# Block products for three of the five down-projection steps at the end of a two-layer decoder step

## The chip, the core and the metric

The program runs on one NeuronCore of a Trainium2 chip. The core has a matrix engine (TensorE, PE in the profile; its weight loads are PEld), VectorE (DVE), ScalarE (ACT), GpSimd (POOL) and SyncE (SP), each with an instruction queue of its own that runs in order, and 16 DMA engines, on which transfers issued from SP, ACT and POOL run. Matmuls write to PSUM, which has 8 banks of 512 f32 per partition. The metric is the device time of one execution in microseconds; less is better.

## The reference

Two groups of tokens (a prompt of 1024 and 8 samples) go through two layers that share all weights. Each layer has a mixer and then a SwiGLU feed-forward block, with norms before and after and a residual sum. What this change touches is the feed-forward block:

```python
def swiglu(h, w_gu, w_down):
    gate, up = jnp.split(h @ w_gu, 2, axis=-1)
    return (jax.nn.silu(gate) * up) @ w_down
...
h = h + rmsnorm(swiglu(rmsnorm(h, g[2]), w_gu[l], w_down[l]), g[3])
```

`w_gu` is 1024 x 5632 and `w_down` 2816 x 1024, in float32.

## The kernel before

Activations lie transposed: features on the 128 partitions, tokens along the free dimension. The tokens are cut into two groups: group 0 holds 512 prompt tokens, group 1 the other 512 and the 8 samples, 520 in all, worked as two halves of `h` = 260. Every float32 product is made as three products of rounded parts: a tile is split into a rounded tile (a cast on ScalarE) and the remainder (a subtraction on VectorE), and high x high, high x low and low x high are added up in PSUM. `split_w` (L196), `split_to` (L226) and `split` in `gate_up_w` (L509) do this for weights and activations; a weight tile of 128 x 512 is 256 KB, loaded on SP's queue.

The 22 feature tiles of 128 are cut into `PARTS` of 5, 5, 4, 4 and 4 (L582). For each part, the gate and up products of its tiles are made, then the part's contribution to the down projection is added to `R`, eight tiles of 128 output features by 520 tokens.

The program's end is the feed-forward block of group 1 in layer 1, class `ffn_w` (L584). Its first four feature tiles are plain (`gate_up_q`, L468). The other 18 go through `gate_up_w` (L493): the 1024 x 2 x 260 problem of one tile's gate and up is seen as 2 x 2 blocks and made with seven products instead of eight (Winograd's form). The seven need four sums of weight blocks, which `weight_sums` (L557) makes earlier, in DRAM, with POOL transfers: plain copies and accumulating ones, eight per part, for all 22 tiles. Each is released by a token, a ScalarE copy of one column of something just computed into a tile of three buffers (tag "rr"), and a POOL copy of that (L571, L572), so the transfers are spread over the feed-forward block of group 0 in layer 1 (L1648 to L1650). They also need sums of activation blocks, made once by `sums_w` (L295).

The down step of a part in `ffn_w.part` (L608) is plain: for each of the eight output tiles it loads and splits the part's rows of `w_down` (two loads where the part has five tiles), makes three matmuls per feature tile and token half (L638), and adds both halves to `R` on VectorE (L647). The fifth part's step is `down_rows` (L651), which works in two groups of tokens, makes the norm's statistics as it goes, and turns the result to rows and stores it.

PSUM in this last part is one pool of four tags with two buffers each, all eight banks (`Q`, L87, L1670). `gate_up_w` takes one bank of each tag, a plain down step two of them for each output tile. Weight buffers come from `spl` and `raws` (L593, L599), which in parts 1 to 4 also borrow from two other pools.

Instructions are put in order by a scheduler with priorities in program order; `weave` (L174) interleaves generators by their weights, and so sets these priorities. In layer 0, the recurrence of group 1 (`a1.core`) is woven with the first feed-forward part of group 0 (`f0.part(0)`) at L1632. At the start, 14 mask tiles `mf` (L1579) are made by POOL in a pool `tpool` of three buffers, and the page table is loaded to a tile of its own (L1609) and made into row indices, which the gathers of L1000 use.

Of the kernel before, what the change touches and what calls it, by code (L numbers as in the profile page):

```python
# [9 lines left out]
F32 = mybir.dt.float32  # L10
# [8 lines left out]
P = 128  # L19
# [5 lines left out]
def tile_decoder(  # L25
# [56 lines left out]
    def N():  # L82
        return npool.tile([P, WID], F32, tag="n", name=nm("n"))
# [14 lines left out]
    def M(dt=F32):  # L98
        return mpool.tile([P, 2, WID], dt, tag="m", name=nm("m"))
# [21 lines left out]
    def small(shape, dt=F32, tag="sm", bufs=None):  # L121
        return spool.tile(shape, dt, tag=tag, name=nm(tag), bufs=bufs)
# [42 lines left out]
    def drain(*gens):  # L165
        for g_ in gens:
            for _ in g_:
                pass
# [5 lines left out]
    def weave(*streams):  # L174
        drain(mixed(*streams))
# [50 lines left out]
    def split_to(dst, src):  # L226
        nc.scalar.copy(dst[0], src)  # L227
        nc.vector.tensor_sub(dst[1], src, dst[0].bitcast(F32))  # L228
# [261 lines left out]
        split_to((mt[:, 0, :n], mt[:, 1, :n]), sg[:, :n])  # L490
        return mt, last

    def gate_up_w(l, f, ops, spl, raws):  # L493

        h, n = PW[1], NG[1]
        part, o = part_of(f)
        gate, up = f * P, DFF + f * P
        src = [
            (w_gu[l][0:512, gate : gate + P], 0), (sums[l][part][0][:, o : o + P], 4), (sums[l][part][1][:, o : o + P], 5),
            (w_gu[l][512:D, gate : gate + P], 1), (sums[l][part][2][:, o : o + P], 6), (sums[l][part][3][:, o : o + P], 2),  # L500
            (w_gu[l][512:D, up : up + P], 3),
        ]

        def weight(j):
            r = raws()
            nc.sync.dma_start(r, src[j][0].rearrange("(k p) m -> p k m", p=P))
            return r.rearrange("p k m -> p (k m)")

        def split(src):  # L509
            w = spl()  # L510
            nc.scalar.copy(w[:, 0, :], src)  # L511
            nc.vector.tensor_sub(w[:, 1, :], src, w[:, 0, :].bitcast(F32))  # L512
            return w

        def product(ps, j, first=False):
            w = split(weight(j))
            i = src[j][1]
            for k in range(4):
                x = ops[k][i]
                for wi, (wj, xi) in enumerate(((0, 0), (0, 1), (1, 0))):  # L520
                    nc.tensor.matmul(  # L521
                        ps[:, :h], w[:, wj, k * P : (k + 1) * P], x[:, xi, :],
                        start=(first and k == 0 and wi == 0), stop=(k == 3 and wi == 2), skip_group_check=True,
                    )
# [6 lines left out]
        nc.scalar.activation(pc[:, :h], pb[:, :h], AF.Copy, scale=-1.0)  # L531
# [12 lines left out]
        nc.vector.tensor_mul(sg[:, :h], sg[:, :h], pb[:, :h])  # L544
        nc.vector.tensor_mul(sg[:, h:n], sg[:, h:n], gt[:, h:n])
        mt = M(F32R)
        split_to((mt[:, 0, :n], mt[:, 1, :n]), sg[:, :n])
        return mt

    sums = {}  # L550
# [3 lines left out]
            if f0 <= f < f0 + nf:  # L554
                return i, (f - f0) * P

    def weight_sums(l, parts, after):  # L557

        for i in parts:
            f0, nf = PARTS[i]  # L560
            w = nf * P
            s1, s2, s3, s4 = (tc.dram_tile([512, w], F32, name=nm("wsum")) for _ in range(4))
            sums.setdefault(l, {})[i] = (s1, s2, s3, s4)
            a11, a12 = (w_gu[l][r : r + 512, f0 * P : f0 * P + w] for r in (0, 512))
            a21, a22 = (w_gu[l][r : r + 512, DFF + f0 * P : DFF + f0 * P + w] for r in (0, 512))
            for d, a, add in (
                (s3, a11, False), (s1, a21, False), (s3, a21, True), (s1, a22, True),
                (s2, s3, False), (s2, a22, True), (s4, s2, False), (s4, a12, True),
            ):
                tok = small([P, 1], tag="rr")  # L570
                nc.scalar.copy(tok, after())  # L571
                mark = nc.gpsimd.tensor_copy(small([P, 1], tag="mk", bufs=1), tok)  # L572
                with tc.issue_after(mark.ins):
                    if add:
                        nc.gpsimd.dma_start(d, a, accum_op=ALU.add)
                    else:
                        nc.gpsimd.dma_start(d, a, max_dma_last_dim=4 * w)
                yield

    htok, done = [], []  # L580

    PARTS = [(0, 5), (5, 5), (10, 4), (14, 4), (18, 4)]  # L582

    class ffn_w:  # L584


        def __init__(self, l, x, plain):
            self.g, self.l, self.x, self.ops, self.plain, self.n, self.r, self.pi = 1, l, x, [], plain, 0, 0, 0
            self.R = self.acc = None
            self.half = []  # L590
            self.sums = sums_w(x, self.ops)

        def spl(self):  # L593
# [12 lines left out]
            return wraw.tile([P, 4, P], F32, tag="w", name=nm("w"))  # L606

        def part(self, pi):  # L608
            l, n, h = self.l, NG[1], PW[1]
            f0, nf = PARTS[pi]  # L610
            last = pi == len(PARTS) - 1
            mids = []
            for j in range(nf):
                self.pi = pi
                if f0 + j < self.plain:
                    mt, ins = gate_up_q(l, f0 + j, self.x)
                    mids.append(mt)
                    with tc.issue_after(ins.ins):
                        for _ in range((1, 2, 1, 0)[j]):
                            next(self.sums, None)  # L620
                else:
                    mids.append(gate_up_w(l, f0 + j, self.ops, self.spl, self.raws))
                yield
            if pi == 0:
                self.R = R_one()
            if last:
                with tc.issue_after(done[-1].ins):
                    nc.scalar.preload_act_table_set("natural_log_exp_and_others")
                yield from self.down_rows(mids, f0, nf)
                return  # L630
            for m in range(ND):
                w = split_w(w_down[l], f0, nf, m * P)
                pp = [Q(2 * (m % 2) + a) for a in range(2)]
                for k in range(nf):
                    wh, wl = w[k]
                    for wi, (wt, xi) in enumerate(((wh, 0), (wh, 1), (wl, 0))):
                        for a in range(2):
                            nc.tensor.matmul(  # L638
                                pp[a][:, :h], wt, mids[k][:, xi, a * h : (a + 1) * h],
                                start=(k == 0 and wi == 0), stop=(k == nf - 1 and wi == 2),  # L640
                            )
                for a in range(2):
                    d = self.R[m][:, a * h : (a + 1) * h]
                    if pi == 0:
                        nc.scalar.copy(d, pp[a][:, :h])
                    else:
                        nc.vector.tensor_add(d, d, pp[a][:, :h])  # L647
                if m % 2:
                    yield
# [960 lines left out]
    nc.sync.dma_start(ptb, page_table.rearrange("b j -> (b j)").partition_broadcast(P))  # L1610
# [95 lines left out]
```

## Time and profile before

| what | value |
|---|---|
| median of 3 runs | 2442.65 us (2439.48 to 2443.6) |
| the profiled execution, its own time | 2441.46 us |
| its span, first to last instruction | 2439.7 us |
| mean granted clock of TensorE | 0.998 |
| packets of DMA, bytes | 496726, 360.33 MB |

The profile is one execution. A line of its views gives the engine, the source line, the operation and the tiles (out <- in), the shapes and the count. Busy times of PE are modelled ends of pipelined matmuls, so the length of a row of matmuls in the chain, divided by their number, is the cost of one. "Idle before" is the time in which an engine stood still before such an instruction, and what ended it. The chain of work that ended last is followed back from the last instruction, at each step to what released it.

### The profile page before, as it was taken

The numbers are of one execution on the slowest core, as the hardware profiler recorded it, in microseconds if no ns is written. First come the engines' busy times: TensorE is split into PE (matmuls) and PEld (weight loads), VectorE is DVE, ScalarE is ACT, GpSimd is POOL, SyncE is SP. The second block draws the span as 40 slices with busy tenths as digits, with TensorE's granted clock in tenths as the row PEclk, the third lists the DMA queues.
The fourth block names the chain that finished last, engine by engine and source line by source line (L and its number), as shares of the span: only waits on it lengthen the run. The fifth ranks groups of instructions, "written<-read, shape, count | busy, mean of one in ns | idle before, by whom it ended". The sixth has DMA issues, their size and how long they took to land.

```text
span 2439.7 us, 40660 instructions
## 1 busy us (share of the span) xinstructions
PE 2410.5 (99%) x15483; PEld 2140.8 (88%) x15483; DVE 1561.0 (64%) x2688; ACT 1205.8 (49%) x2371; POOL 106.3 (4%) x167
## 2 busy tenths in 40 slices
PE   8999999999999999999999999999999999999998
PEld 6888988888877887999999989877787898999998
DVE  5777556765775676555544585677678548755665
ACT  5547544444444454555433454555454445554445
POOL 3000000000000000011111100021000000000000
PEclk9999999999999999999999999999999999999999
DMA  6353252254643446685778966544454234474542
GB/s 189 97 157 107 74 156 84 71 172 121 181 135 95 139 147 209 175 222 149 181 198 211 247 183 193 162 146 136 127 156 130 81 121 125 125 195 144 151 140 75
DMA packets 496726, 360.33 MB, mean 148 GB/s; under 512 B 19181, under 2 KB 443738, under 8 KB 496530
## 3 DMA queue, kind: packets, MB, share of 16 engines
q1 hardware_dynamic: 477864, 303.15, 41.7%
q0 software_dynamic: 18560, 54.53, 9.3%
q8 instruction: 122, 2.00, 0.3%
q14 instruction: 74, 0.61, 0.1%
q10 hardware_dynamic: 106, 0.04, 0.0%
HBM read 327.83 MB, written 75.96 MB: 166 GB/s over the span
## 4 chain that ended last, share of the span: by engine, by line
PE 92%; DVE 3%; DMA 2%; ACT 1%; issue 1%; SPq 0%; DVEq 0%; ACTq 0%; POOLq 0%; POOL 0%
PE mm L220 63%; PE q L521 7%; PE q L638 4%; PE q L479 2%; PE mm L1064 2%; PE s L914 1%; PE s L873 1%; PE s L1422 1%; PE s L1247 1%; PE mm L850 1%; PE q L722 1%; PE s L1461 1%; PE mm L823 1%; PE s L900 1%; DMA b<-qd 1%
## 5 line engine op out<-in xcount | busy, mean ns | idle before, releaser
L220 PE MATMUL mm<-x,ws 128*128 128x260 f32 (+1 forms) x7776 | 1330.5, 330 | 0.0
L220 PEld LDWEIGHTS mm<-x,ws 128*128 128x128 f32 x7776 | 1149.4, 188 | 143.1 <-issue 8.0
L206 ACT CAST ws<-w 128x512 fp32r<-128x512 f32 x704 | 414.8, 590 | 674.0 <-PE mm L220 556.4
L207 DVE TENSOR_TENSOR ws<-w,ws 128x512 fp32r<-128x512 f32 x704 | 456.6, 652 | 259.9 <-ACT ws L206 254.8
L220 PE MATMUL mm<-m,ws 128*128 128x512 f32 (+1 forms) x2112 | 391.9, 342 | 0.3 <-DVE r L416 0.3
L220 PEld LDWEIGHTS mm<-m,ws 128*128 128x128 f32 x2112 | 323.3, 188 | 47.0 <-issue 3.3
L512 DVE TENSOR_TENSOR ws<-w,ws 128x512 fp32r<-128x512 f32 x126 | 86.5, 691 | 59.7 <-ACT ws L511 57.0
L521 PE MATMUL q<-y,ws 128*128 128x260 f32 x864 | 112.9, 283 | 0.0
L511 ACT CAST ws<-w 128x512 fp32r<-128x512 f32 x126 | 78.0, 621 | 68.2 <-PE q L638 27.3
L521 PEld LDWEIGHTS q<-y,ws 128*128 128x128 f32 x864 | 107.6, 188 | 0.0
L638 PE MATMUL q<-m,ws 128*128 128x260 f32 x864 | 104.7, 282 | 0.0
L638 PEld LDWEIGHTS q<-m,ws 128*128 128x128 f32 x864 | 103.8, 188 | 0.3 <-ACT hT L454 0.2
L416 DVE TENSOR_TENSOR r<-r,mm 128x512 f32<-128x512 f32 (+1 forms) x96 | 66.0, 688 | 56.6 <-PE mm L220 55.5
L260 DVE TENSOR_SCALAR t<-mm 128x512 f32<-128x512 f32 (+1 forms) x74 | 51.2, 691 | 63.7 <-PE mm L220 63.7
L770 DVE TENSOR_TENSOR t<-t,mm 128x512 f32<-128x512 f32 (+1 forms) x66 | 45.5, 690 | 67.8 <-PE mm L220 67.2
L264 DVE TENSOR_TENSOR t<-t,t 128x512 f32<-128x512 f32 (+1 forms) x66 | 45.8, 693 | 65.7 <-ACT t L263 65.7
L521 PE MATMUL q<-x,ws 128*128 128x260 f32 x648 | 86.3, 282 | 0.0
L521 PEld LDWEIGHTS q<-x,ws 128*128 128x128 f32 x648 | 81.3, 188 | 0.0
L227 ACT CAST m<-t 128x512 fp32r<-128x512 f32 (+1 forms) x88 | 54.9, 624 | 24.7 <-DVE t L770 16.7
L1000 POOL DMA_INDIRECT c<-in_cache_sb_k,pidx x16 | 16.7, 1042 | 1120.8 <-DMA vsc<-c 910.9
L283 DVE TENSOR_TENSOR st<-st,n 128x512 f32<-128x512 f32 (+1 forms) x91 | 62.2, 691 | 3.1 <-ACT n L282 1.5
L228 DVE TENSOR_TENSOR m<-t,m 128x512 fp32r<-128x512 f32 (+1 forms) x88 | 60.9, 692 | 2.8 <-ACT m L227 1.6
(356 smaller groups left out, 2579.9 us busy)
## 6 DMA issues: line engine op xcount, KB each, us to landing
w<-in_w_gu SPq DMA_DIRECT2D x334, 256.0 KB, 3.3
w<-in_w_down SPq DMA_DIRECT2D x160, 256.0 KB, 2.9
w<-in_w_in_a SPq DMA_DIRECT2D x80, 256.0 KB, 2.9
wsum<-in_w_gu POOLq DMA_DIRECT2D x18, 1024.0 KB, 9.3
w<-wsum SPq DMA_DIRECT2D x72, 256.0 KB, 3.8
w<-in_w_o SPq DMA_DIRECT2D x64, 256.0 KB, 2.8
wsum<-in_w_gu POOLq DMA_DIRECT2D x12, 1280.0 KB, 10.9
w<-in_w_mem_kv SPq DMA_DIRECT2D x32, 256.0 KB, 3.2
```

The source lines that it names most:

```text
L206: nc.scalar.copy(ws[:, 0, :n, :], raw[:, :n, :])
L207: nc.vector.tensor_sub(ws[:, 1, :n, :], raw[:, :n, :], ws[:, 0, :n, :].bitcast(F32))
L220: nc.tensor.matmul(ps[:, a, : PW[g]], wt, xt[k][:, xi, o : o + PW[g]], start=(k == 0 and wi == 0), stop=(k == nk - 1 and wi == 2),)
L227: nc.scalar.copy(dst[0], src)
L228: nc.vector.tensor_sub(dst[1], src, dst[0].bitcast(F32))
L260: nc.vector.tensor_scalar(sv(x, g), pv(ps, g), -44.0, None, op0=ALU.max)
L283: nc.vector.tensor_add(acc[:, :n], acc[:, :n], t[:, :n])
L416: nc.vector.tensor_add(dst, dst, pv(ps, g))
L511: nc.scalar.copy(w[:, 0, :], src)
L512: nc.vector.tensor_sub(w[:, 1, :], src, w[:, 0, :].bitcast(F32))
L521: nc.tensor.matmul(ps[:, :h], w[:, wj, k * P : (k + 1) * P], x[:, xi, :], start=(first and k == 0 and wi == 0), stop=(k == 3 and wi == 2), ...
L638: nc.tensor.matmul(pp[a][:, :h], wt, mids[k][:, xi, a * h : (a + 1) * h], start=(k == 0 and wi == 0), stop=(k == nf - 1 and wi == 2),)
```

## The change

The down steps of parts 1, 2 and 3 go to a new method `down_w`, which sees the first four feature tiles of the part as two blocks of rows, the 1024 output features as two blocks of columns and the tokens as two halves, and makes seven products. It runs in two passes of two output tiles (and the two that lie 512 features further); each pass takes all eight PSUM banks. The fifth tile of part 1 is added by plain matmuls (`slice_of`).

The activation sums that this needs are made in `gate_up_w` at the end of the second tile of each pair (`put_sum`), in place and in a pool whose tiles grow from 2048 to 2080 bytes. The weight sums of `w_down` are made in DRAM by `down_sums`, 24 POOL transfers of 512 KB, woven with `a1.core` and `f0.part(0)` in layer 0. `weight_sums` leaves out the columns of the four plain tiles. In the last part, the gate and up of the next part's first tile is put ahead of the down steps of parts 2 and 3. The page table and an index tile move to `tpool`.

```diff
-    def gate_up_w(l, f, ops, spl, raws):
+    def gate_up_w(l, f, ops, spl, raws, pair=None):
...
-        sg = T()
+        sg = T() if pair is None else N()
...
         mt = M(F32R)
+
+        def put_sum(dst, d, a, b):
+            nc.vector.tensor_sub(d, a, b)
+            split_to((dst[:, 0], dst[:, 1]), d)
+
+        if not pair:
+            w = n if pair is None else h
+            split_to((mt[:, 0, :w], mt[:, 1, :w]), sg[:, :w])
+            if pair is not None:
+                put_sum(mt[:, :, h:n], sg[:, :h], sg[:, h:n], sg[:, :h])
+                pair.append((mt, sg))
+            return mt
+        m0, s0 = pair.pop()
         split_to((mt[:, 0, :n], mt[:, 1, :n]), sg[:, :n])
+        y = [bpool.tile([P, 2, h], F32R, tag="b", name=nm("ys")) for _ in range(3)]
+        put_sum(y[2], s0[:, h:n], s0[:, h:n], sg[:, h:n])
+        put_sum(y[1], sg[:, h:n], sg[:, h:n], s0[:, :h])
+        put_sum(y[0], sg[:, :h], sg[:, :h], sg[:, h:n])
+        pair.extend((m0[:, :, :h], mt[:, :, :h], mt[:, :, h:n], y[0], m0[:, :, h:n], y[1], y[2]))
         return mt
...
-    def weight_sums(l, parts, after):
+    def weight_sums(l, parts, after, plain=0):
...
+            skip = max(0, plain - f0) * P
...
+            yield from summed((s1, s2, s3, s4), a11, a12, a21, a22, after)
+
+    def down_blocks(l, f0):
+        rows = w_down[l][f0 * P : (f0 + 4) * P, :].rearrange("(t s p) m -> s p t m", s=2, p=P)
+        return [rows[i][:, :, o : o + 512] for o in (0, 512) for i in range(2)]
+
+    def down_sums(l, parts, after):
+        for i in parts:
+            t = [tc.dram_tile([P, 2, 512], F32, name=nm("dsum")) for _ in range(4)]
+            dsums[i] = t
+            yield from summed(t, *down_blocks(l, PARTS[i][0]), after)
+
+    def summed(t, a11, a12, a21, a22, after):
+        s1, s2, s3, s4 = t
+        for d, a, add in (
+            (s3, a11, False), (s1, a21, False), (s3, a21, True), (s1, a22, True),
+            (s2, s3, False), (s2, a22, True), (s4, s2, False), (s4, a12, True),
+        ):
+            tok = small([P, 1], tag="rr")
+            nc.scalar.copy(tok, after())
+            mark = nc.gpsimd.tensor_copy(small([P, 1], tag="mk", bufs=1), tok)
+            with tc.issue_after(mark.ins):
+                if add:
+                    nc.gpsimd.dma_start(d, a, accum_op=ALU.add)
+                else:
+                    nc.gpsimd.dma_start(d, a, max_dma_last_dim=4 * 512)
+            yield
...
+        def down_w(self, pi, f0, pairs, extra):
...
+            src = ((a11, 0), (s1, 4), (s2, 5), (a12, 1), (s3, 6), (s4, 2), (a22, 3))
+            for m0 in (0, 2):
+                ms = (m0, m0 + 1)
+                acc = [[Q(i) for i in range(4)] for _ in ms]
+
+                def weight(rows):
+                    r = self.raws().rearrange("p k m -> p (k m)")
+                    nc.sync.dma_start(r.rearrange("p (t c) -> p t c", t=2), rows[:, :, m0 * P : (m0 + 2) * P])
+                    w = self.spl()
+                    split_to((w[:, 0, :], w[:, 1, :]), r)
+                    return w
...
+                def product(q, j, first=False):
+                    w = weight(src[j][0])
+                    for i in range(2):
+                        for t in range(2):
+                            x = pairs[t][src[j][1]]
+                            o = t * 256 + i * P
+                            for wi, (wj, xi) in enumerate(((0, 0), (0, 1), (1, 0))):
+                                nc.tensor.matmul(
+                                    acc[i][q][:, :h], w[:, wj, o : o + P], x[:, xi, :],
...
+                def add(q, mo, a, sub=False):
+                    for i, m in enumerate(ms):
+                        d = R[m + mo][:, a * h : (a + 1) * h]
+                        (nc.vector.tensor_sub if sub else nc.vector.tensor_add)(d, d, acc[i][q][:, :h])
+
+                def minus(q, p):
+                    for i in range(2):
+                        nc.scalar.activation(acc[i][q][:, :h], acc[i][p][:, :h], AF.Copy, scale=-1.0)
+
+                product(0, 0, True)
+                minus(1, 0)
+                product(3, 1, True)
+                product(1, 2)
+                minus(2, 1)
+                product(0, 3)
+                if extra:
...
+                    slice_of(0, 0, 0)
+                add(3, 4, 1)
+                add(0, 0, 0)
+                product(1, 4)
+                add(3, 0, 1, True)
+                add(1, 4, 1)
+                product(2, 5)
+                if extra:
+                    slice_of(2, 0, 1)
+                add(2, 0, 1)
+                product(1, 6)
+                if extra:
+                    slice_of(1, 1, 0)
+                    slice_of(0, 1, 1, True)
+                    add(0, 4, 1)
+                add(1, 4, 0)
+                yield
...
-    ptb = const.tile([P, NB * NP], I32, name="ptb")
+    ptb = tpool.tile([P, NB * NP], I32, tag="t", name="ptb")
...
-    iot = const.tile([P, NB * NP], I32, name="iot")
+    iot = tpool.tile([P, NB * NP], I32, tag="t", name="iot")
...
-    weave((a1.core(), 22), (f0.part(0), 9))
+    weave((a1.core(), 22), (f0.part(0), 9), (down_sums(1, (1, 2, 3), lambda: f0.now), 24))
...
-    ws = weight_sums(1, range(5), lambda: f1.now)
+    ws = weight_sums(1, range(5), lambda: f1.now, 4)
...
-    drain(f1.part(2), f1.part(3), f1.part(4))
+    drain(f1.gate_up(2), f1.gate_up(3, 0, 1), f1.down(2), f1.gate_up(3, 1))
+    drain(f1.gate_up(4, 0, 1), f1.down(3), f1.gate_up(4, 1), f1.down(4))
```

More of the change, by code (lines that the diff above doesn't have):

```diff
@@ L563, in weight_sums @@
             sums.setdefault(l, {})[i] = (s1, s2, s3, s4)
[L564 to L578, printed above, removed]
+            c0, c1 = f0 * P + skip, f0 * P + w
@@ new lines, in weight_sums @@
+            a11, a12 = (w_gu[l][r : r + 512, c0:c1] for r in (0, 512))
+            a21, a22 = (w_gu[l][r : r + 512, DFF + c0 : DFF + c1] for r in (0, 512))
+            s1, s2, s3, s4 = (t[:, skip:w] for t in (s1, s2, s3, s4))
+            yield from summed((s1, s2, s3, s4), a11, a12, a21, a22, after)
+    def down_blocks(l, f0):
+        rows = w_down[l][f0 * P : (f0 + 4) * P, :].rearrange("(t s p) m -> s p t m", s=2, p=P)
+        return [rows[i][:, :, o : o + 512] for o in (0, 512) for i in range(2)]
@@ L580, in tile_decoder @@
+    dsums = {}
     htok, done = [], []
@@ L589, in __init__ @@
             self.R = self.acc = None
-            self.half = []
+            self.half, self.mids = [], {}
             self.sums = sums_w(x, self.ops)
@@ L608, in part, with block, gate_up @@
         def part(self, pi):
+            yield from self.gate_up(pi)
+            yield from self.down(pi)
+        def block(self, pi):
+            return 0 < pi < len(PARTS) - 1
+        def gate_up(self, pi, j0=0, j1=None):
             l, n, h = self.l, NG[1], PW[1]
             f0, nf = PARTS[pi]
-            last = pi == len(PARTS) - 1
-            mids = []
-            for j in range(nf):
+            mids, pairs = self.mids.setdefault(pi, ([], ([], [])))
+            for j in range(j0, nf if j1 is None else j1):
                 self.pi = pi
@@ L621, in part, with slice_of @@
                 else:
-                    mids.append(gate_up_w(l, f0 + j, self.ops, self.spl, self.raws))
+                    pair = pairs[j // 2] if self.block(pi) and j < 4 else None
+                    mids.append(gate_up_w(l, f0 + j, self.ops, self.spl, self.raws, pair))
                 yield
+        def down_w(self, pi, f0, pairs, extra):
+            l, n, h, R = self.l, NG[1], PW[1], self.R
+            a11, a12, a21, a22 = down_blocks(l, f0)
+            s1, s2, s3, s4 = dsums[pi]
+            src = ((a11, 0), (s1, 4), (s2, 5), (a12, 1), (s3, 6), (s4, 2), (a22, 3))
[8 more added lines that the diff above has]
+                    return w
+                def slice_of(q, hf, a, first=False):
+                    for i in range(2):
+                        o = hf * 256 + i * P
+                        for wi, (wj, xi) in enumerate(((0, 0), (0, 1), (1, 0))):
+                            nc.tensor.matmul(
+                                acc[i][q][:, :h], we[:, wj, o : o + P], extra[0][:, xi, a * h : (a + 1) * h],
+                                start=(first and wi == 0), stop=(wi == 2), skip_group_check=True,
+                            )
+                def product(q, j, first=False):
[4 more added lines that the diff above has]
+                            o = t * 256 + i * P
+                            for wi, (wj, xi) in enumerate(((0, 0), (0, 1), (1, 0))):
+                                nc.tensor.matmul(
+                                    acc[i][q][:, :h], w[:, wj, o : o + P], x[:, xi, :],
+                                    start=(first and t == 0 and wi == 0), stop=(t == 1 and wi == 2),
+                                    skip_group_check=True,
+                                )
+                def add(q, mo, a, sub=False):
[3 more added lines that the diff above has]
+                def minus(q, p):
+                    for i in range(2):
+                        nc.scalar.activation(acc[i][q][:, :h], acc[i][p][:, :h], AF.Copy, scale=-1.0)
[6 more added lines that the diff above has]
+                if extra:
+                    tail = w_down[l][(f0 + 4) * P : (f0 + 5) * P, :].rearrange("p (o m) -> p o m", o=2)
+                    we = weight(tail)
+                    slice_of(0, 0, 0)
[15 more added lines that the diff above has]
+                yield
@@ L624, in part, with down @@
+        def down(self, pi):
+            l, n, h = self.l, NG[1], PW[1]
+            f0, nf = PARTS[pi]
+            last = pi == len(PARTS) - 1
+            mids, pairs = self.mids.pop(pi)
             if pi == 0:
@@ L629, in part @@
                 yield from self.down_rows(mids, f0, nf)
+                return
+            if self.block(pi):
+                yield from self.down_w(pi, f0, pairs, mids[4:])
                 return
```

## The prediction

> **What bounds the kernel now.** I read the page first, then the chain of work that ended last, cut to the last 340 us, then the waits of TensorE there, then busy time by stretch.
>
> ```profile
> span 2439.7 us, 40660 instructions
> ...
> PE 2410.5 (99%) x15483; PEld 2140.8 (88%) x15483; DVE 1561.0 (64%) x2688; ACT 1205.8 (49%) x2371; POOL 106.3 (4%) x167
> ```
>
> TensorE (PE) is busy for 99% of the span, so only fewer or shorter matmuls can shorten it, or a new hole can lengthen it. The change edits the last part, which the chain shows in order of time (start, length, what, instructions):
>
> ```profile
> 2156.51 50.43 PE q L521 x420
> 2206.94 28.70 PE q L638 x240
> 2235.64 40.34 PE q L521 x336
> 2275.99 22.99 PE q L638 x192
> 2298.98 40.37 PE q L521 x336
> 2339.36 23.03 PE q L638 x192
> 2362.39 38.92 PE q L521 x324
> ```
>
> Each piece starts where the one before it ends: from 2156.5 to 2401.3 us the path is TensorE alone. L521 is gate/up (five, four, four, four feature tiles, 84 matmuls each), L638 the down steps of parts 1, 2 and 3. A matmul costs 22.99 / 192 = 0.120 us in a down step and 40.34 / 336 = 0.120 in gate/up. The wait view of TensorE from 2040 us to the end has one row, and it is earlier than these pieces:
>
> ```profile
> PE q L479 <- DVE r L416: 1.7, 1, 1.7
> ```
>
> The stretches of part 2, gate/up then down (length, PE, PEld, DVE, ACT and POOL busy, clock, DMA share, GB/s), show how much room VectorE (DVE) and ScalarE (ACT) have beside it:
>
> ```profile
> 2235.60:2276.00 40.40, 40.40 (x339) 40.40 (x338) 26.65 (x48) 24.32 (x50) 0.00 (x0) 1.00 0.62 179
> 2276.00:2299.00 23.00, 23.00 (x194) 23.00 (x194) 12.86 (x27) 6.22 (x10) 0.00 (x0) 1.00 0.42 117
> ```
>
> **Term 1: the matmuls that go.** By the code, a down step over four feature tiles now takes 8 output tiles x 4 x 3 x 2 = 192 matmuls of 260 columns. Seven block products in two passes take 2 x 7 x 12 = 168, of the same width, operand type and weight loads. Part 1 has a fifth tile, done plainly: 240 becomes 168 + 48 = 216. That is 3 x 24 = 72 matmuls less, and 72 x 0.120 = 8.6 us. The three steps become 25.9, 20.2 and 20.2 us.
>
> **Term 2: what VectorE and ScalarE do instead.** Rows of the down stretch, then of the gate/up stretch, then the 260-wide sums that the kernel already makes at L295 (busy, mean ns of one | idle before):
>
> ```profile
> L647 DVE TENSOR_TENSOR r<-r,q 128x260 f32<-128x260 f32 x15 | 5.7, 421 | 7.7 <-PE q L638 7.7
> L512 DVE TENSOR_TENSOR ws<-w,ws 128x512 fp32r<-128x512 f32 x6 | 4.2, 692 | 1.6 <-ACT ws L511 1.4
> L511 ACT CAST ws<-w 128x512 fp32r<-128x512 f32 x6 | 3.7, 622 | 9.1 <-PE q L638 7.5 <-DMA w<-in_w_gu 0.9 <-DMA w<-wsum 0.7
> ```
>
> ```profile
> L228 DVE TENSOR_TENSOR m<-t,m 128x520 fp32r<-128x520 f32 x3 | 2.1, 702 | 0.0
> L531 ACT ACTIVATE q<-q 128x260 f32<-128x260 f32 x4 | 1.5, 372 | 2.9 <-PE q L521 2.9
> ```
>
> ```profile
> L317 DVE TENSOR_TENSOR b<-b,b 128x260 f32<-128x260 f32 x16 | 6.7, 419 | 0.0
> L228 DVE TENSOR_TENSOR y<-b,y 128x260 fp32r<-128x260 f32 x16 | 6.7, 418 | 0.0
> L227 ACT CAST y<-b 128x260 fp32r<-128x260 f32 x16 | 6.6, 410 | 3.9 <-DVE b L317 3.8
> ```
>
> A four-tile down step was 8 weight splits and 16 adds on VectorE, 8 x 0.692 + 16 x 0.421 = 12.3 us of 23.0. It becomes 14 splits and 24 adds: 14 x 0.692 + 24 x 0.421 = 19.8 us of 20.2, which is 98%. ScalarE: 14 x 0.622 + 8 copies of 0.372 = 11.7 us. A pair of feature tiles had two 520-wide remainders, 1.40 us on VectorE; it becomes one such, one 260-wide and four sums of two instructions, 0.70 + 9 x 0.42 = 4.5, so 3.1 us more. Two pairs put the gate/up stretch at 26.65 + 6.2 = 32.8 us of 40.4. Over a whole part that is 52.6 us of 60.5, 87%: VectorE stays under TensorE, though barely in the down steps. The casts at L511 waited 7.5 us for TensorE and 1.6 for transfers, so ScalarE runs as far ahead as the weight buffers let it; this lead covers a short backlog. The 14 loads per 20.2 us have gate/up's rate (28 per 40.4), at which the DMA share is 0.62 and no wait of TensorE is listed. I cost all this at nothing; without the lead, each add or copy that frees a bank is paid (rival A).
>
> Of the 8 banks a pass takes all. Behind each minus (ScalarE) and each add that frees a bank stands another product of 12 matmuls, 1.44 us, against 2 x 0.372 or 2 x 0.421 plus the hand-over. The exception is part 1: its pass ends with the plain slice, and the next product wants that bank. The first add (0.42) plus hand-overs, less the 0.36 us in which the slice's second half runs, is 0.3 us; with a split ahead of it (0.69) 1.0. It happens twice: 0.6 to 2.0, of which I take 1.0 as splits are half of VectorE's work there. Gate/up of the next part's first tile, moved ahead of the down steps of parts 2 and 3, gives the last pair's sums 10.1 us of cover; their chain is about 0.42 + 0.42 + 0.62 + 0.70 + 3 x 1.25 = 5.9 us. For part 1 the fifth tile does it. The two-buffer tile that the paired SiLU goes to is wanted again four products (5.8 us) into the next tile, about when that chain ends; what queues behind it on ScalarE is the copy of the second bank and the casts. 0 to 3 us, I take 0.
>
> **Term 3: the sums of w_down in DRAM.** 24 POOL transfers of 512 KB, each released by a ScalarE copy and a POOL copy, run beside the first down-projection part of group 0, about 396 to 490 us:
>
> ```profile
> wsum<-in_w_gu POOLq DMA_DIRECT2D x18, 1024.0 KB, 9.3
> ...
> wsum<-in_w_gu POOLq DMA_DIRECT2D x12, 1280.0 KB, 10.9
> wsum<-wsum POOLq DMA_DIRECT2D x6, 1024.0 KB, 7.3
> ```
>
> ```profile
> 408.52 0.62 ACT L227 CAST m<-t 128x512 fp32r<-128x512 f32 x1
> ...
> 420.51 0.62 ACT L227 CAST m<-t 128x512 fp32r<-128x512 f32 x1
> ...
> 487.31 0.59 ACT L414 COPY r<-mm 128x512 f32<-128x512 f32 x1
> ```
>
> By the slope between the first two rows (1.6 us per 256 KB) 512 KB lands in 6.1 us. Six of a part's eight transfers form a chain, some 30 us with the issues, 90 us for three parts. By the interleaving the 24 tokens come in twos and threes, one burst per feature tile (408.5, 420.5) and then per two output tiles, the last at 487: 4 us apart on average. POOL is thus nearly full, but a burst of three has drained when the next comes. The token has three buffers: ScalarE stops only when POOL is three steps behind, and then the casts behind it stop. At 6.1 us this costs 0; at the 1 MB price of 9.3 the last bursts hold ScalarE for about 7 us, less the lead of four weight buffers, 2.8 us each (12 matmuls of 0.235, Term 4). Bounds 0 to 7, taken 0.
>
> The Trainium skill's "DMA: Bandwidth & Descriptors" (Anatomy of one DMA) fits such a transfer as 2.0 us plus bytes / 436e3, an estimate of 3.2 us for 512 KB; the 1 MB rows show twice its figure, so the rows stand. By it this term would be 0 with room to spare.
>
> What gate/up's own sums lose (four fifths of the first part's eight transfers) ran beside a busy TensorE:
>
> ```profile
> 985.00:1200.00 215.00, 213.33 (x1690) 206.22 (x1689) 119.96 (x219) 111.07 (x247) 21.56 (x34) 1.00 0.71 180
> ```
>
> so they give back nothing, 1.7 us at the very most; the new cap of 2048 on the copies' last dimension, where it was 4w, has the same answer.
>
> **Term 4: the page table's tile at the start.** It moves into the three-buffer pool behind 14 mask tiles, so its load on SP's queue waits for POOL:
>
> ```profile
> 5.41 0.33 SPq L1610 DMA_DIRECT2D ptb<-in_page_table  x1
> 6.46 2.23 SPq L1056 DMA_DIRECT2D w<-in_w_in_a  x5
> ...
> 13.18 3.07 SPq L1056 DMA_DIRECT2D w<-in_w_in_a  x3
> ```
>
> ```profile
> 8.14 0.54 POOL L1581 TENSOR_SCALAR_AFFINE_SELECT mf<-ones 128x64 f32<-128x64 f32 x1 [3.27 <-PE s L145]
> ...
> 21.34 0.43 POOL L1585 TENSOR_SCALAR_AFFINE_SELECT mf<-mf 128x64 f32<-128x64 f32 x2
> ```
>
> ```profile
> 13.76 1.89 PE L1064 MATMUL mm<-ws,x 128*128 128x512 f32 x4
> ...
> 21.09 17.62 PE L1064 MATMUL mm<-ws,x 128*128 128x512 f32 x75
> ```
>
> The masks end near 21 us. Queued behind the load are the weights that ScalarE casts for L1064. If it holds only the sixth weight on (13.18), they land by 25 us, and TensorE, with 75 matmuls of 0.235 us left at 21.1, wants the sixth weight at 21.1 + 39 x 0.235 = 30: nothing. If it went ahead of the first five, TensorE would lose up to 8 us; if it goes behind more loads, 0.4 is gained. I take 0: by POOL's rows the third of 14 mask tiles starts at 8.1 us, when the five loads are already going out, and the page table's tile comes after all of them.
>
> **Sum**, on the profiled execution's own 2441.46 us (span 2439.7): 2441.5 - 8.6 + 1.0 = 2433.9. The three runs shown have their median 1.2 us above that execution (2442.65), so I forecast 2435.
>
> **Rivals.** A, slower: the banks' hand-overs are paid. A pass has four (two minus copies, the add before the seventh product, the change of pass), six passes 24. For: all eight banks are in use and VectorE is 98% loaded, in order, so an add that has lost its cover waits for a split of 0.69 us; with every one paid, 24 x 0.7 = 16.8 us and 2452. Against: the 1.44 us behind each, and a mean load of 87%. It decides from 8.6 / 24 = 0.36 us per hand-over.
>
> B, gain given back: POOL's chain holds ScalarE in the front (7 us), or the start pays (8): 2442 to 2443. For: POOL nearly full there, VectorE too:
>
> ```profile
> 420.00:440.00 20.00, 20.00 (x107) 16.86 (x107) 19.91 (x39) 8.12 (x16) 0.00 (x0) 1.00 0.17 50
> ```
>
> Against: 24 tokens spread over 90 us and ScalarE 41% busy. "SBUF — State Buffer" of the Trainium skill, in its trap of VectorE blocking DMA, has POOL's descriptor writing locked out by some VectorE modes. It speaks against this change, and by it the figure is B's; no run here yet shows such a wait.
>
> C, VectorE sets the pace in the down steps: at 10% idle in its order 22 us a step, 1.8 longer than TensorE, three times: 5.4 us, 2440. Against: work that has piled up does not wait for operands.
>
> **How the numbers follow.** Forecast 0.64, A 0.20, B 0.10, C 0.06. About 0.2%, 4.9 us, can be told from no change here: faster is all of the forecast and a third of C (0.66), same is B and the rest of C, (0.14), slower is A (0.20). The forecast's own range is 2432 (no refill, runs 1 us low) to 2438 (3 us for the SiLU tile). To hold 8 in 10 the range goes to 2450, through B and C and the lower half of A.
>
> **What would show it.** Right: 15411 matmuls; down steps in the chain of 26, 20 and 20 us with no idle of TensorE but about half a microsecond at part 1's pass ends; VectorE near 95% there; ScalarE's token copies without waits on POOL; L1064 still starting near 13.8 us. Wrong: waits of the block products on the adds or minus copies (A), idle of TensorE between 400 and 510 us (B), or splits late behind adds (C).

## The result, and the profile after

| | median us | lowest to highest | runs |
|---|---|---|---|
| kernel before | 2441.09 | 2437.53 to 2444.66 | 20 |
| changed kernel | 2445.34 | 2443.12 to 2448.4 | 20 |

The ratio is 1.0015, with a 95% interval of [1.0009, 1.0022]: the change makes the kernel slower by 4.25 us. The time lies inside the predicted range, but it moved to the other side of before than the forecast of 2435.

The page of the changed kernel gives the same picture as before: TensorE busy for 99% of the span, with exactly the number of matmuls that was forecast.

```profile
span 2441.4 us, 40853 instructions
...
PE 2405.5 (99%) x15411; PEld 2134.9 (87%) x15411; DVE 1596.0 (65%) x2776; ACT 1231.6 (50%) x2455; POOL 137.0 (6%) x215
```

So TensorE has 5.0 us less work (2410.5 before) and yet the span is 1.7 us longer. The chain of waits, cut to the last 350 us, shows the edited part (start, length, what, instructions):

```profile
2166.15 50.46 PE q L521 x420
2216.61 5.77 PE q L700 x48
...
2242.77 50.54 PE q L521 x420
2293.31 20.13 PE q L700 x168
2313.44 40.37 PE q L521 x336
2353.81 20.06 PE q L700 x168
2373.87 28.82 PE q L521 x240
```

L700 holds the block products, L688 the plain slice of part 1. The three down steps take 2242.77 - 2216.61 = 26.16, 20.13 and 20.06 us, 66.35 in all. Before they took 28.70 + 22.99 + 23.03 = 74.72, so 8.37 us are gained, as forecast, and each piece starts where the one before it ends. But the first row of this list stood at 2156.51 before and stands at 2166.15 now: the kernel comes to its last part 9.64 us late. That is the whole loss: 9.64 - 8.37 = 1.27 us, and the rest of the path is 0.4 us longer, which makes the 1.7 us of the spans. (The medians differ by 4.25 us. The profiled execution of the changed kernel, 2443.12 us, is the fastest of its 20.)

The place is the start. TensorE's waits in the first 60 us begin with two rows, the second of which the same view of before doesn't have (waiting engine, tile and line, releaser, then us in total, times, longest):

```profile
PE s L145 <- DMA prow<-in_hg_norm: 7.9, 1, 7.9
PE ns L365 <- DVE x L369: 6.4, 1, 6.4
```

The first matmul after the first projection gives the delay there. Before and after, in the timeline of TensorE (start, length, engine, line, what, count):

```profile
40.17 1.92 PE L1081 MATMUL s<-a,flip 128*128 128x256 f32 x8
```

```profile
50.31 1.90 PE L1207 MATMUL s<-a,flip 128*128 128x256 f32 x8
```

It is 10.1 us late at 50 us. The chain of the changed kernel, cut to its first 60 us, tells why:

```profile
20.35 0.19 POOL mf L1711
20.55 0.16 SPq L1736
20.71 0.04 issue
20.75 3.38 DMA w<-in_w_in_a
24.14 0.02 issue
24.16 0.63 ACT ws L1184
24.79 0.02 issue
24.81 0.69 DVE ws L1185
25.50 0.67 DVE x L369
26.18 0.04 issue
26.22 1.11 PE ns L365 x4
```

To be read downwards. POOL's masks give a buffer of `tpool` free at 20.5 us; now SP can issue the page table's load (L1736), and behind it in SP's queue the next weight load; the weight lands at 24.1, ScalarE casts it, VectorE makes its remainder and then the remainder of an operand tile `x`, and only then can TensorE go on. The chain before has neither POOL nor a weight load in this stretch: it comes from the token loads of the first microseconds to the first operands, and is TensorE alone from 13.76 us on. The queue itself, in the timeline of SP:

```profile
5.06 2.92 SPq L1182 DMA_DIRECT2D w<-in_w_in_a  x4
20.38 0.33 SPq L1736 DMA_DIRECT2D ptb<-in_page_table  x1
20.75 0.91 SPq L1182 DMA_DIRECT2D w<-in_w_in_a  x2
```

Four weight loads go out, then the page table's load waits for 12.4 us (5.06 + 2.92 = 7.98 to 20.38), and all the others wait behind it. What stands behind the fifth weight on ScalarE shows in that engine's timeline; the last field is the idle time before, and what ended it:

```profile
11.64 1.77 ACT L1184 CAST ws<-w 128x512 fp32r<-128x512 f32 x3
13.76 0.69 ACT L368 ACTIVATE x<-ns,par 128x512 fp32r<-128x512 f32 x1 [0.35 <-PE ns L365]
14.35 0.68 ACT L368 ACTIVATE x<-s,par 128x512 fp32r<-128x512 f32 x1
24.16 0.62 ACT L1184 CAST ws<-w 128x512 fp32r<-128x512 f32 x1 [9.13 <-DMA w<-in_w_in_a]
24.68 0.68 ACT L368 ACTIVATE x<-ns,par 128x512 fp32r<-128x512 f32 x1
```

ScalarE stands still for 9.13 us, with the cast of the fifth weight (L1184) at the head of its queue. The copies of the third and later operand tiles (L368) are queued behind that cast. TensorE's next transposes wait for these (the wait of 6.4 us above ends with an `x` of L369), while it needs the fifth weight only later: by the code each weight serves 12 matmuls, so the fifth is wanted after 48, and 9 are done. So the page table's tile, 0.33 us of issue, holds a load, the load holds a cast, and the cast holds operands that have nothing to do with it.

The hole is 6.4 of the 10.1 us. Another part goes with the clock that TensorE was granted. The window from 23 to 29 us, before and after (length, PE, PEld, DVE, ACT and POOL busy, clock, DMA share, GB/s):

```profile
23.00:29.00 6.00, 6.00 (x27) 4.85 (x26) 2.49 (x4) 1.39 (x3) 0.00 (x0) 1.00 0.96 328
```

```profile
23.00:29.00 6.00, 2.78 (x9) 2.39 (x10) 2.92 (x5) 3.40 (x6) 0.49 (x2) 0.50 1.01 341
```

The granted clock is 1.00 before and 0.50 here. The four transposes and eight matmuls behind the hole take 1.11 + 2.79 = 3.9 us in the chain; at the rates of the chain before (0.44 us for four transposes, 17.38 / 75 for a matmul) they would take 2.3. So some 1.6 us goes with the lower clock. It is 0.50 in the other trace with the hole too (experiment 2, from 24 to 30 us), and 1.00 from 14 to 40 us in every trace without it; what lowers it, no run here tells. The remaining 2 us lie ahead of the hole, and executions without any hold differ there as well: in their eight traces the matmul above starts between 39.83 and 41.55 us.

### The profile page after: what moved, and what is told of

It is laid out like the page before. It is cut to its first block, busy times and chain, and to the rows that moved or that the text cites. A ratio compares the mean times of both kernels' runs of the same rounds, so it can differ in the third digit from the quotient of the medians.

```text
span 2441.4 us, 40853 instructions
## 1 busy us (share of the span) xinstructions
PE 2405.5 (99%) x15411; PEld 2134.9 (87%) x15411; DVE 1596.0 (65%) x2776; ACT 1231.6 (50%) x2455; POOL 137.0 (6%) x215
## 4 chain that ended last, share of the span: by engine, by line
PE 92%; DVE 3%; DMA 2%; ACT 1%; issue 1%; POOL 0%; SPq 0%; ACTq 0%; DVEq 0%; POOLq 0%
PE mm L220 63%; PE q L521 7%; PE q L700 2%; PE q L479 2%; PE mm L1190 2%; PE s L1040 1%; PE q L764 1%; PE s L999 1%; PE s L1548 1%; PE s L1373 1%; PE mm L976 1%; PE q L848 1%; PE s L1587 1%; PE mm L949 1%; PE s L1026 1%
## 5 line engine op out<-in xcount | busy, mean ns | idle before, releaser
L206 ACT CAST ws<-w 128x512 fp32r<-128x512 f32 (+1 forms) x672 | 397.5, 593 | 647.9 <-PE mm L220 555.6
L207 DVE TENSOR_TENSOR ws<-w,ws 128x512 fp32r<-128x512 f32 (+1 forms) x672 | 438.1, 655 | 237.8 <-ACT ws L206 231.0
L512 DVE TENSOR_TENSOR ws<-w,ws 128x512 fp32r<-128x512 f32 x126 | 86.6, 691 | 46.5 <-ACT ws L511 44.3
L511 ACT CAST ws<-w 128x512 fp32r<-128x512 f32 x126 | 77.8, 618 | 47.7 <-PE q L521 15.2
L607 POOL COPY mk<-rr 128x1 f32<-128x1 f32 x64 | 30.2, 472 | 751.1 <-ACT rr L606 751.1
L261 ACT ACTIVATE t<-t 128x512 f32<-128x512 f32 (+1 forms) x66 | 41.9, 635 | 40.5 <-DVE t L260 36.3
L227 ACT CAST m<-t 128x512 fp32r<-128x512 f32 (+1 forms) x76 | 47.4, 624 | 25.6 <-DVE t L896 18.5
L228 DVE TENSOR_TENSOR m<-t,m 128x512 fp32r<-128x512 f32 (+1 forms) x76 | 52.6, 692 | 2.2 <-ACT m L227 0.9
```

What stands on the lines that cost most here:

```text
L206: nc.scalar.copy(ws[:, 0, :n, :], raw[:, :n, :])
L207: nc.vector.tensor_sub(ws[:, 1, :n, :], raw[:, :n, :], ws[:, 0, :n, :].bitcast(F32))
```

## The experiments

The expectations name theories by letters: S is the start just described, F the narrower claim that the hold costs only by way of the fifth weight's cast in ScalarE's queue, D a loss by the 24 new sums of `w_down` in DRAM, V a down step that has no room left on VectorE. Times are medians, in places with lowest and highest; ratios are to the kernel before, run beside them, with a 95% interval. It had 2441.12 us beside experiments 1 to 4, 2439.59 beside 5, 7, 8 and 9, and 2440.94 beside 6, so between these groups the ratios compare better than the times.

**1. The changed kernel, with the two tiles in a pool that nobody holds.**

```diff
-    ptb = tpool.tile([P, NB * NP], I32, tag="t", name="ptb")
+    ptb = apool.tile([P, NB * NP], I32, tag="a", name="ptb")
...
-    iot = tpool.tile([P, NB * NP], I32, tag="t", name="iot")
+    iot = apool.tile([P, NB * NP], I32, tag="a", name="iot")
```

> The changed kernel with the page table's tile and the index tile in a pool that is empty at that moment, so that the load waits for no buffer. Theory S (the start pays: SP's queue stands behind the page table's load until POOL has made its masks, about 10 us): 2445.3 - 10.1 = 2435, that is about 6 us under the kernel before; matmuls of L1190 start before 14.5 us and run on without the 6.4 us hole; in the tail the down steps stay 26, 20 and 20 us. Theory D (the DRAM sums of w_down cost the time in layer 0): no more than 2 us better than the changed kernel. Theory T (the block products' gain in the tail is not real in runs without a profile): 2441, level with the kernel before.

Measured: 2434.67 us (2432.64 to 2436.82), ratio 0.9971 [0.996, 0.9982]. TensorE's wait of 6.4 us is gone, and SP's queue has the page table early, with all five weights behind it at once:

```profile
5.02 0.43 SPq L1736 DMA_DIRECT2D ptb<-in_page_table  x1
6.91 2.23 SPq L1182 DMA_DIRECT2D w<-in_w_in_a  x5
```

One buffer's place is worth 2445.34 - 2434.67 = 10.7 us, and without it the rest of the change is a gain of 6.4 us (5.0 to 6.4 over the three repairs, with experiments 4 and 5). This kernel beats both the kernel before and the changed one.

**2. The kernel before, with only those two tiles moved to `tpool`.** The edit is the one in the change's own diff: `const` becomes `tpool` for `ptb` and `iot`.

> The kernel before with nothing but the two tiles moved into the three-buffer pool. Theory S: 2441.1 + 10 = 2451, with the fifth weight load after 20 us and a hole of about 6 us before L365's transposes. Theory D: 2441. Theory T: 2445, the start's share of the changed kernel's loss and nothing more.

Measured: 2451.96 us (2450.24 to 2452.57), ratio 1.004 [1.0027, 1.0054]: 10.8 us slower than the kernel before (2441.12 in these runs). The hole is there without any of the block products; TensorE's waits have it:

```profile
PE ns L365 <- DVE x L369: 6.0, 1, 6.0
```

Put in and taken out, the same edit costs the same: the start is shown as the cause.

**3. The kernel before, with the 24 transfers of the `w_down` sums beside layer 0, their results unused.**

```diff
+    def down_sums(l, parts, after):
...
-    weave((a1.core(), 22), (f0.part(0), 9))
+    weave((a1.core(), 22), (f0.part(0), 9), (down_sums(1, (1, 2, 3), lambda: f0.now), 24))
```

> The kernel before with the 24 transfers of w_down sums added beside the recurrence of group 1, their results not used. Theory S: 2441, within 1 us of the kernel before; no wait of ScalarE on POOL over 1 us between 400 and 510 us. Theory D: 2445 or more, with ScalarE's token copies waiting on POOL.

Measured: 2442.76 us, ratio 1.0006 [0.9997, 1.0015]. It can't be told from nothing; the interval allows 0.15%, 3.7 us, at most. The median is 1.6 us above and not within the 1 us that S named, but of ScalarE's waits between 400 and 510 us none is on POOL. Theory D falls: the sums don't hold what the block products gain. Put together, 10.8 (run 2) + 1.6 (this run's median, 2442.76 - 2441.12) - 8.4 (the down steps) = 4.0 us agrees with what the whole change costs, 4.25; the middle term is not told from zero.

**4. The changed kernel, with the page table loaded from POOL's queue.**

```diff
-    nc.sync.dma_start(ptb, page_table.rearrange("b j -> (b j)").partition_broadcast(P))
+    nc.gpsimd.dma_start(ptb, page_table.rearrange("b j -> (b j)").partition_broadcast(P))
```

> The changed kernel with the page table's load issued from POOL's queue in place of SP's; the tiles stay in the three-buffer pool. Theory S: the wait stays, but stands behind nothing that matters, so 2435 as in the first run. If the pool itself (its buffers missing to someone else) were the cost, 2445 as in the changed kernel.

Measured: 2435.12 us, ratio 0.9978 [0.9969, 0.9987]. The tile waits for its buffer as long as ever: POOL issues the load only at 20.96 us, when its masks are done but for the last two casts.

```profile
20.96 0.75 POOL L1736 DMA_DIRECT2D ptb<-in_page_table  x1
```

So the late page table costs nothing that can be seen by itself. What cost 10 us was what stood behind it in SP's queue.

**5. The changed kernel, with the page table's block of seven lines written ahead of the mask loop** (same pool, same queue).

> The changed kernel with the page table's lines put ahead of the mask tiles, in the same three-buffer pool. Theory S (the cost is the wait for a buffer behind the masks, not the pool): the load waits for nothing and stands third on SP's queue; 2435. Rival (the masks, with a buffer less for a while, end late and hold something): more than 2440.

Measured: 2434.59 us, ratio 0.9977 [0.9965, 0.9988], no hole at the start. The tile then takes the first of the three buffers, and its load goes out at 4.57 us. This is the third repair that comes to the same time, and it keeps the saving of memory.

**6. The changed kernel, with the page table's block one step later**, so that its load stands behind the fifth weight load and not ahead of it.

```diff
-    ptb = tpool.tile([P, NB * NP], I32, tag="t", name="ptb")
...
     drain(start(0, x0))
     a0 = mixer_a(0, x0)
-    drain(a0.v(), a0.fq())
+    drain(a0.v())
+    ptb = tpool.tile([P, NB * NP], I32, tag="t", name="ptb")
...
+    drain(a0.fq())
```

> The changed kernel with the page table's lines traced after the first projection, so that its load stands one place further back on SP's queue, behind the fifth weight load and ahead of the sixth; the tiles stay in the three-buffer pool and the wait for the masks stays. ScalarE's order of casts and copies at the start is the same as in the changed kernel. Theory F (the hold costs because ScalarE has the fifth weight's cast ahead of the copies that make the third to sixth operand tiles; the sixth's cast stands behind these): loss at most 1 us, 2435 to 2436, the load still held until about 20 us. Rival (SP's queue standing still costs by itself, whichever weights are behind): 2441 to 2445.

Measured: 2436.29 us (2434.0 to 2439.88), ratio 0.9982 [0.9973, 0.9991]. The page table's load is held as long as in the changed kernel, to 20.75 us, but now five weights are out before it. SP's queue, then ScalarE:

```profile
5.33 2.86 SPq L1182 DMA_DIRECT2D w<-in_w_in_a  x5
20.75 0.33 SPq L1739 DMA_DIRECT2D ptb<-in_page_table  x1
```

```profile
15.26 0.62 ACT L1184 CAST ws<-w 128x512 fp32r<-128x512 f32 x1
17.81 0.69 ACT L368 ACTIVATE x<-ns,par 128x512 fp32r<-128x512 f32 x1 [1.93 <-PE ns L365]
...
24.76 0.62 ACT L1184 CAST ws<-w 128x512 fp32r<-128x512 f32 x1 [3.15 <-DMA w<-in_w_in_a]
```

The fifth weight's cast runs at 15.26, the operand copies behind it follow, and it is the sixth weight that waits. TensorE's hole of 6.4 us is gone, and the first matmul after the projection starts at 42.38 us, where the changed kernel has 50.31 and the kernel before 40.17. Theory F holds, with its 2435 to 2436 missed by 0.3 us and the rival's 2441 by 4.7: a hold of the same length, one place further back in the queue, costs 2.2 us at that point and not 10, and 0.8 against the latest of the traces without a hold (41.55). Of the two ways in which ScalarE could have been held, by the loads as such or by the one cast that stands ahead of the operand copies, it is the second.

The three other runs ask what the block products' side work would cost if its cover were gone; all stand on the kernel of the first experiment (2434.67 us).

**7. The next part's first tile not moved ahead of the down steps.**

```diff
-    drain(f1.gate_up(2), f1.gate_up(3, 0, 1), f1.down(2), f1.gate_up(3, 1))
-    drain(f1.gate_up(4, 0, 1), f1.down(3), f1.gate_up(4, 1), f1.down(4))
+    drain(f1.part(2), f1.part(3), f1.part(4))
```

> The first repair (page table's tiles in an empty pool) with the parts of the tail in plain order again: no gate/up tile of the next part ahead of the down steps of parts 2 and 3. Theory C (that tile covers the last pair's sums): their chain of about 5.9 us is late behind two products that need none of it (2.9 us), so TensorE loses about 3 us at each of two steps, 2434.7 + 6 = 2441, with waits of the block products on the sums. Rival (the scheduler and the weight lead cover it anyway): 2434.7, no such waits.

Measured: 2435.51 us, ratio 0.9977 [0.9968, 0.9987]; no loss that can be told from experiment 1 (0.9971), and the same ratio as experiment 5. I had priced this cover at 3 us in each of two steps. The chain at part 2's down step:

```profile
2276.72 3.34 PE q L700 x28
2280.06 0.03 issue
2280.09 17.01 PE q L700 x140
```

The step takes 3.34 + 0.03 + 17.01 = 20.4 us and not 20.1, with VectorE busy for 19.88 of it. The last pair's sums come while the first products, which don't need them, run: their first user is the third product, and the path leaves TensorE for 0.03 us. The claim that the moved tile is needed as cover falls.

**8 and 9. More work for VectorE in the down steps**: a second computation of 260, or of all 512, columns of each weight's remainder, 44 times.

```diff
                     split_to((w[:, 0, :], w[:, 1, :]), r)
+                    nc.vector.tensor_sub(w[:, 1, :260], r[:, :260], w[:, 0, :260].bitcast(F32))
```

> The first repair with 260 columns of each weight remainder of the block down steps computed a second time: 0.42 us more on VectorE for each of 44 weight tiles. VectorE then has about 25 us of work in a step of 20.1. Theory V (VectorE is just under the pace, and the weights split ahead cover only a short excess): 4 to 5 us over per four-tile step and 1.5 in part 1, less what the lead covers, 2435 to 2445, with the first waits of the block products on their split weights. Rival (it was far from mattering, the order has slack): 2434.7.

> The same with all 512 columns again: 0.69 us more for each of 44 weight tiles, about 28.3 us of VectorE in a step of 20.1. Theory V: 8 us over per four-tile step and 6 in part 1, 22 together, less the lead: 2443 to 2457, VectorE without idle in the down steps. Rival: under 2440.

Measured: 2435.01 us, ratio 0.998 [0.9968, 0.9991], with 260 columns; 2436.36, ratio 0.9982 [0.9973, 0.9992], with 512. The second dose, in the view of groups (busy, mean ns of one | idle before), is

```profile
L682 DVE TENSOR_TENSOR ws<-w,ws 128x512 fp32r<-128x512 f32 x44 | 29.6, 684 | 0.0
```

29.6 us by the records; VectorE's busy time from part 1's gate/up to the end of part 4's grows by 206.73 - 184.82 = 21.9, as records of neighbouring instructions overlap. It costs 1.7 us by the medians and 2.7 by the ratios (0.9982 against 0.9971), and the intervals overlap, so not even that is told from nothing. V expected the step to be paced by VectorE, and its 2443 to 2457 is missed. The windows of the second dose tell why; they are the gate/up stretch before part 2's down step, that step, and the gate/up stretch behind it (length, PE, PEld, DVE, ACT and POOL busy, clock, DMA share, GB/s):

```profile
2274.70:2284.70 10.00, 10.00 (x85) 10.00 (x85) 10.00 (x22) 7.30 (x16) 0.00 (x0) 1.00 0.49 148
2284.70:2306.60 21.90, 21.07 (x174) 20.74 (x174) 21.17 (x47) 11.96 (x24) 0.00 (x0) 1.00 0.37 109
2306.60:2336.90 30.30, 30.30 (x255) 30.30 (x254) 25.85 (x51) 19.76 (x43) 0.00 (x0) 1.00 0.83 238
```

Without a dose (experiment 1) VectorE's busy time in the first stretch was 8.87 of 10.2 us, in the down step 18.65 of 20.2 and in the third 22.36 of 30.2. The down step's splits begin in the stretch before, and gate/up's own splits, some of which ran ahead during the down step, move into the stretch behind (27 there for 21 without a dose). So the load that counts is that of the three together. With the first two stretches full, a wait appears in TensorE's list, and it is a single one, in a step that is 1.8 us longer (21.9 for 20.1):

```profile
PE q L701 <- DVE ws L682: 0.8, 1, 0.8
```

## Why the prediction was wrong

**The step that failed is Term 4, the start, which the sum took as 0.** The prediction found the right mechanism (the tile behind 14 masks, its load at the head of SP's queue until POOL ends near 21 us; measured 20.4) and mis-sized it. Two things in it were wrong.

First, whom it asks. "Queued behind the load are the weights that ScalarE casts for L1064" was right, but the cost was then worked out from when TensorE *wants* a weight: the sixth at 30 us, so nothing is lost. The weight's cast is an instruction in ScalarE's queue, which runs in order, and the copies at L368 that make TensorE's operands stand behind it. The deadline that counts is the one of whatever is next in *that* queue, and for the fifth weight it is between 15.0 us, where ScalarE's idle time of 9.13 us begins, and about 17.2: in experiment 6 the next copy starts at 17.81, as its operands come no earlier, and the cast takes 0.62. It ran at 24.16. The trace of before already showed the order, in ScalarE's timeline: the casts of the third to fifth weights, then the third operand tile's copy.

```profile
14.18 1.66 ACT L1058 CAST ws<-w 128x512 fp32r<-128x512 f32 x3
16.13 0.69 ACT L368 ACTIVATE x<-ns,par 128x512 fp32r<-128x512 f32 x1 [0.29 <-PE ns L365]
```

Second, where the load stands. The argument "the page table's tile comes after all of them" took it from the time at which the third mask tile starts; the load is queued between the fourth and the fifth weight. The prediction considered "sixth on" (0) and "ahead of the first five" (8), and the truth lay between them in place, yet beyond both in price: 10.1 us in the trace, 10.8 in experiment 2 and 10.7 in experiment 1. Nor did it count the 0.50 of the clock behind the hole, 1.6 us of the 10.1. Experiment 6 shows what the case of "sixth on", taken as 0, costs: 1.6 us by the medians (2436.29 against 2434.67) and 2.7 by the ratios, too close to be told from nothing.

**Term 1 was right**: 72 matmuls less, 8.37 us measured for 8.6 forecast, steps of 26.2, 20.1 and 20.1 us for 25.9, 20.2 and 20.2.

**Term 2 was too cautious.** The 1.0 us for the hand-over of banks at part 1's pass ends wasn't paid; TensorE has no wait there. VectorE, put at 98% of a down step, is busy for 18.55 of 20.1 us, 92%:

```profile
2293.30:2313.40 20.10, 20.10 (x170) 20.10 (x169) 18.55 (x42) 11.90 (x24) 0.00 (x0) 1.00 0.65 186
```

and it would have borne more: "barely" was wrong by the 22 us of experiment 9, and the cover of the tile moved ahead isn't needed (experiment 7).

**Term 3 was right.** The sums landed in 6.2 us (third number, after count and KB), for an estimate of 6.1 from the slope of larger ones:

```profile
dsum<-in_w_down POOLq DMA_DIRECT2D x18, 512.0 KB, 6.2
```

The 3.2 us that the fit in the Trainium skill's "DMA: Bandwidth & Descriptors" (Anatomy of one DMA) gives is not borne out, as the 1 MB rows had said. The trap in the Trainium skill's "SBUF — State Buffer" (VectorE blocking DMA) spoke against these transfers; no wait of that kind shows, and experiment 3 puts the price of all 24 between -0.03% and 0.15%. VectorE was busy for 19.9 us of the 20 from 420 us there, and for 8 to 16 of the 20 in the windows from 440 to 500.

**The rivals.** A and C (hand-overs paid, VectorE as the pace) didn't occur. B named the start at 8 us and so 2442 to 2443, with a chance of 0.10; its second half is what happened, with a price a quarter to a third higher. With Term 4 taken out, experiment 1 gives 2434.67 us where the forecast said 2435. That agreement is partly luck. The forecast started from 2442.65, 1.5 us above the median of 20, and of the 8.37 us that the down steps gain, 6.4 (2441.12 - 2434.67, interval 0.18 to 0.40%, 4.4 to 9.8 us) show in the medians. Experiments 4 and 5 gained 6.0 and 5.0, and the interval of experiment 4 (0.13 to 0.31%, 3.2 to 7.6 us) leaves 8.37 out. So something of the change seems to cost 2 to 3 us outside the edited part. Whether that is the DRAM sums (1.6 us in experiment 3, not told from zero) stays open; single traces can't tell, as the last part begins at 2159.88, 2157.16 and 2155.75 us in experiments 1, 4 and 5, and at 2156.51 before.

## What to carry to other kernels

When a load is put behind a wait on a shared in-order queue, list what stands behind it there, and then what stands behind each of those loads' first users on *their* engine's queue: the deadline is that of the next instruction in the queue, not that of the data. A tile taken from a rotating pool comes only when an earlier user lets a buffer go, however small the tile; here two tiles of 64 bytes per partition ate a gain of 8 us. A side edit of a large change deserves a run of its own, and so does its repair: another pool, another queue or an earlier place in the program all gave 2434.6 to 2435.1 us.

## What the runs showed that I had not expected

- A held transfer's price jumps with its place in the queue. One place ahead of the fifth weight load: 10.7 us. One place behind it, held equally long: 1.6 to 2.7, not told from nothing.
- After a hole of 6 us TensorE worked at a granted clock of 0.50 for some microseconds, in both traces that have the hole, so the loss was larger than the wait.
- A late start isn't absorbed later. 10.1 us lost at 50 us is still 9.64 us at 2166 (in experiment 2, 11.1 and 10.6), in a kernel whose engines other than TensorE are 65% busy at most; TensorE is 92% of the chain.
- A stage with an engine 92% busy took another 7 us of that engine's work per step on average (21.9 us over three) at a cost of 1.7 to 2.7 us in all, not told from nothing, as work moved to the stages on both sides.
